# Factors per token spread over the partitions by two small transfers instead of products with the identity

## The chip, the cores and the metric

The kernel runs on one core of a Trainium2 chip. The metric is the device time of one execution in microseconds (us); the time before is 2590.07 us, the median of three runs (2589.15 to 2590.61).

The core has five engines with instruction streams of their own: TensorE (PE in the profile: products of 128-row tiles; PEld is its loading of weights), VectorE (DVE), ScalarE (ACT), GpSimd (POOL) and SyncE (SP). SyncE issues nearly all transfers between memory (DRAM) and the on-chip SBUF. Products land in PSUM, which VectorE and ScalarE read.

## The reference

Two layers on a sequence of 1024 tokens with 1024 features, float32: forgetting attention and then retention, each followed by a gated feed-forward network (FFN), with an RMS norm ahead of each of the four parts and one at the end.

```python
def rmsnorm(x, g):
    y = x * lax.rsqrt(jnp.mean(x * x, axis=-1, keepdims=True) + EPS)
    return y * g

for i in range(2):
    h = rmsnorm(x, norm_mix[i])
    x = x + (forgetting_attention(h, ...) if i == 0 else retention(h, ...))
    h = rmsnorm(x, norm_ffn[i])
    x = x + swiglu(h, ...)
return rmsnorm(x, final_norm)

# retention, per head (4 heads, value width 512), y from the chunked scan:
mu = jnp.mean(y, axis=-1, keepdims=True)
var = jnp.mean(jnp.square(y - mu), axis=-1, keepdims=True)
y = (y - mu) * lax.rsqrt(var + EPS)          # one factor per token
out = (silu(g) * y) @ w_out
```

Each norm has one factor per token, which multiplies that token's whole row of features.

## The kernel before

Activations are kept transposed: features on the 128 partitions, tokens along the free dimension, in two halves of 512 tokens (`HALF`). A factor per token must therefore stand in every partition, as a row of 512 values.

**From sums to factors.** The sum of squares of a token is a product with a column of ones (`colsum`, L159), which puts four blocks of 128 tokens as columns: a tile of 128 x 4 with tokens on the partitions. `rsqrt` takes the factor with a square root on ScalarE, a reciprocal on VectorE and a step of refinement (L144 to L153). `rows` (L165) then turns the column into rows: for each of the four blocks, the column is broadcast to 128 x 128 and multiplied by the identity `ident`, so that each partition gets the same 128 factors. It fills a PSUM tile `rw`. The products are in float32, and each is two records in the trace.

**Who uses it.** `rms` runs in four places: in forgetting attention (fox), in the retention's gates when the first pair comes, and in both FFNs at the first gated tile. Each time, it handles two halves, keeps the factor's column `rcol`, and ScalarE copies `rw` to the SBUF row `R` (L178). The first uses of `R` are L232 in fox, L823 in the FFNs and L964 in the gates. `finish` runs eight times in the retention, for four heads and two halves: it copies the head's output tiles to SBUF (`yt`), sums their squares in `yacc` (L1126), makes the factor `yf` (L1135), and VectorE multiplies the four tiles by `rw` straight from PSUM (L1138). For head 0 it also loads four gate tiles `g` and multiplies by them (L1141, L1142). It stores the tiles to memory as `zd` (L1143), from where the output projection loads them. The final norm calls `rows` too (three times, L874); it is left as it is.

**Around a finish.** The retention goes through eight stages of a head and a half. In each, TensorE computes the next stage's scores (L1074 to L1076) and this stage's weighted values (L1100 to L1102). Every operand of a product is split into a high and a low part (`split`, L98 on ScalarE and L99 on VectorE; the scores also through `atd`, L1085, and `wl`, L1090), and a product is made of three. VectorE also centres the values that come from memory (`vd`, L1011). Tiles of 128 x 512 for such work (`yt`, `sq`, `g`) come from a pool of 16 buffers through `yu`.

**What sets the order.** Every engine runs its own list in order. The lists come from a scheduler, which simulates the program's text before the build, so a change in one place reorders what follows. SyncE's list holds 950 transfers; an entry that waits for its data holds all transfers behind it.

Of the kernel before, what the change touches and what calls it, by code (L numbers as in the profile page):

```python
# [10 lines left out]
F32 = mybir.dt.float32  # L11
# [6 lines left out]
P = 128  # L18
# [19 lines left out]
def trunk(ctx, tc, nc, d, out):  # L38
    cp = ctx.enter_context(tc.tile_pool(name="cp", bufs=1))
    yp = ctx.enter_context(tc.tile_pool(name="yp", bufs=16))  # L40
    dp = ctx.enter_context(tc.tile_pool(name="dp", bufs=1, space=DRAM))
# [10 lines left out]
    R = cp.tile([P, S], F32, tag="R", name="R")  # L52
    cnt = [0]

    def nm(s):
        cnt[0] += 1
        return f"{s}_{cnt[0]}"

    def small(shape, tag, bufs=2):
        return (fp if tag[:2] == "f_" else cp).tile(shape, F32, tag=tag, name=nm(tag), bufs=bufs)  # L60
# [4 lines left out]
    mp = ctx.enter_context(tc.tile_pool(name="mp", bufs=1, space=PSUM))  # L65
    banks = [0]

    def mm_ps():
        tag, n = (("mm", 3), ("st", 2), ("pv", 2), ("mm", 3), ("st", 2), ("pv", 2), ("mm", 3))[banks[0] % 7]
        banks[0] += 1  # L70
        return mp.tile([P, H], F32, tag=tag, name=nm("mm"), bufs=n)

    def yu(s):
        return yp.tile([P, H], F32, tag="y", name=nm(s))
# [35 lines left out]
    HALF = (slice(0, H), slice(H, S))  # L110
# [31 lines left out]
    def rsqrt(v, n, r2=None):  # L142
        sd = small([P, n], "rs_a")
        nc.scalar.activation(sd, v, AF.Sqrt)  # L144
        r = small([P, n], "rs_b")
        nc.vector.reciprocal(r, sd)
        t = small([P, n], "rs_c")
        nc.vector.tensor_tensor(t, r, r, op=ALU.mult)
        nc.vector.tensor_tensor(t, t, v, op=ALU.mult)
        nc.vector.tensor_scalar(t, t, -0.5, 1.5, op0=ALU.mult, op1=ALU.add)  # L150
        if r2 is None:
            r2 = small([P, n], "rs_d")
        nc.vector.tensor_tensor(r2, r, t, op=ALU.mult)  # L153
        return r2

    def colsum(acc, mp, mtag, nb=4):
        ps = mp.tile([P, H], F32, tag=mtag, name=nm("cs"))
        for b in range(nb):
            nc.tensor.matmul(ps[:, b:b + 1], acc[:, b * P:(b + 1) * P], ones[:, 0:1], start=True, stop=True)  # L159
        return ps  # L160

    def rows(col, mp, mtag, nb=4):
        ps = mp.tile([P, H], F32, tag=mtag, name=nm("rw"))
        for b in range(nb):
            nc.tensor.matmul(ps[:, b * P:(b + 1) * P], col[:, b:b + 1].to_broadcast([P, P]), ident,  # L165
                             start=True, stop=True)
        return ps

    def rms(norm, mp, mtag, halves=(0, 1)):
        rc = small([P, TB], "rcol", 2)  # L170
        for h in halves:
            ps = colsum(norm.acc[h], mp, mtag)
            v = small([P, 4], "rv")
            nc.vector.tensor_scalar(v, ps[:, 0:4], 1.0 / D, EPS, op0=ALU.mult, op1=ALU.add)
            rsqrt(v, 4, rc[:, 4 * h:4 * h + 4])
        for h in halves:
            ps = rows(rc[:, 4 * h:4 * h + 4], mp, mtag)
            nc.scalar.copy(R[:, HALF[h]], ps)  # L178
        return rc

    xd = [dp.tile([P, S], F32, tag=f"xd{k}", name=f"xd{k}") for k in range(KT)]
# [3 lines left out]
    with ExitStack() as fs:  # L185
# [232 lines left out]
        for h in range(2):  # L418
            ks.append([fp.tile([P, S], F32R, tag=t, name=nm(t)) for t in ("kh", "kl")])
            for b in range(2):  # L420
                tag, n = (("mm", 3), ("mm", 3), ("st", 2), ("st", 2))[2 * h + b]
# [10 lines left out]
        with tc.issue_after(fed.ins):  # L432
            for kt in range(KT):
                for h in range(2):
                    norm.square(h, x0[kt][h])
        rc = rms(norm, mp, "ms")
        tri = const("tri", [P, P])
        bf = cp.tile([P, FOX_HEADS], F32, tag="bf", name="bf")
# [26 lines left out]
        for i, (n, b) in enumerate(TILES):  # L465
            if i < 3:
                mm_u(ops[n, b], wo[n][6:], last_o[:1], b, first=False, last=(i < EVAC))
            else:
                if n == len(wo):
                    wo.append(wtile(d["fox_o"][n][:, :7 * P], 7))  # L470
                tag, bufs = TAGS[i]
# [30 lines left out]
    class Combos:  # L502
# [27 lines left out]
        def finish(self):  # L530
            for n in self.rest[0]:
                for j in range(4):
                    self.t[n][j] = bsplit(self.pools[n], self.rest[j][n])
# [280 lines left out]
    def ffn(i, X, nrm, xold, xnew, last, nw, pools):  # L814
# [4 lines left out]
        def gated(f, c11, c12, c21, c22):  # L819
            if f == 0:  # L820
                rms(nrm, mp, "ms")
            t = yu("t")
            nc.vector.tensor_tensor(t, c11, R[:, HALF[0]], op=ALU.mult)  # L823
            nc.scalar.activation(t, t, AF.Silu)
            nc.vector.tensor_tensor(c12, c12, R[:, HALF[1]], op=ALU.mult)
            nc.scalar.activation(c12, c12, AF.Silu)
            nc.vector.tensor_tensor(t, c21, t, op=ALU.mult)
            nc.vector.tensor_tensor(c22, c22, c12, op=ALU.mult)
            if f < 16:
                if f % 2 == 0:  # L830
                    even.append((t, c22))
                else:
                    stored[f // 8].put(f % 8 // 2, even.pop(), (t, c22))
                return
            nc.vector.tensor_tensor(t, t, R[:, HALF[0]], op=ALU.mult)
            nc.vector.tensor_tensor(c22, c22, R[:, HALF[1]], op=ALU.mult)
            nc.sync.dma_start(ad[f - 16][:, HALF[0]], t)
            nc.sync.dma_start(ad[f - 16][:, HALF[1]], c22)
# [45 lines left out]
    for n in range(KT):  # L884
# [3 lines left out]
        for b in range(2):  # L888
            if (n, b) in ops:
                ps = ops[n, b]  # L890
            elif n < NPART:
                ps = mp.tile([P, H], F32, tag=("pv", "st")[b], name=nm("mm"), bufs=2)
            else:
                ps = mm_ps()
# [64 lines left out]
    def gates(p, c11, c12, c21, c22):  # L959
        if p == 0:  # L960
            rcs.append(rms(nrm, mp, "ms"))
        for k, h, c in ((0, 0, c11), (0, 1, c12), (1, 0, c21), (1, 1, c22)):
            o = c if h else yu("o")
            nc.vector.tensor_tensor(o, c, R[:, HALF[h]], op=ALU.mult)  # L964
            nc.scalar.activation(o, o, AF.Silu)
            nc.sync.dma_start(gd[2 * p + k][:, HALF[h]], o)
# [24 lines left out]
    rc = rcs[0]  # L991
# [123 lines left out]
    def finish(h, ib, yps):  # L1115
        acc = sp.tile([P, H], F32, tag="sacc", name=nm("yacc"), bufs=2)
        ys = []
        for vt in range(4):
            y = yu("yt")
            nc.scalar.copy(y, yps[vt])  # L1120
            if vt == 0:
                nc.scalar.activation(acc, y, AF.Square)
            else:
                sq = yu("sq")
                nc.scalar.activation(sq, y, AF.Square)
                nc.vector.tensor_tensor(acc, acc, sq, op=ALU.add)  # L1126
            ys.append(y)
        cs = colsum(acc, mp, "ms")
        var = small([P, 4], "yv")
        rs = slice(4 * ib, 4 * ib + 4)  # L1130
        nc.vector.scalar_tensor_tensor(var, cs[:, 0:4], 1.0 / 512, rho2[:, h, rs], op0=ALU.mult, op1=ALU.mult)
        nc.vector.tensor_scalar(var, var, EPS, None, op0=ALU.add)
        r = rsqrt(var, 4)
        fac = small([P, 4], "yf")
        nc.vector.tensor_tensor(fac, r, rho[:, h, rs], op=ALU.mult)  # L1135
        fb = rows(fac, mp, "ms")
        for vt in range(4):
            nc.vector.tensor_tensor(ys[vt], ys[vt], fb, op=ALU.mult)  # L1138
            if h < 1:
                g = yu("g")  # L1140
                nc.sync.dma_start(g, gd[4 * h + vt][:, HALF[ib]])  # L1141
                nc.vector.tensor_tensor(ys[vt], ys[vt], g, op=ALU.mult)  # L1142
            nc.sync.dma_start(zd[4 * h + vt][:, HALF[ib]], ys[vt])  # L1143
# [5 lines left out]
    for i, (h, ib) in enumerate(stages):  # L1149
        nxt = stages[i + 1] if i < 7 else None  # L1150
        if ib == 1 and nxt:
            prepare(h + 1)
        yps = [mm_ps() for _ in range(4)]
        if ib == 1:
            crossed(h, yps)
        an = []
        for dg in range(4):
            if nxt:
                an.append(scores(*nxt, dg))
            weighted(h, ib, dg, a[dg], yps)  # L1160
        a = an
        finish(h, ib, yps)
        if ib == 1 and nxt:
            heads[h + 1][4] = state(heads[h + 1][1], heads[h + 1][3])
# [4 lines left out]
    for n in range(KT):  # L1169
        w = wtile2(d["ret_o"][n], 8)  # L1170
        for h in range(2):
            ps = mm_ps()
# [101 lines left out]
```

## Time and profile before

| | |
|---|---|
| median of three runs | 2590.07 us |
| profiled execution | 2592.81 us |
| its span | 2591.0 us |
| granted TensorE clock | 0.997 |
| TensorE busy | 2562.7 us, 99% |
| VectorE, ScalarE busy | 71%, 47% |

The profile is of one execution. Durations of neighbouring instructions on an engine overlap, above all TensorE's, so the time that one takes is read from its start to the next one's start. A timeline row gives start and duration, and in brackets how long the engine stood idle ahead of it and what released it. A row of the waits gives total, times and longest. In views that group rows, `x` is the number of instructions.

### The profile page before, as it was taken

The numbers are of one execution on the slowest core, as the hardware profiler recorded it, in microseconds if no ns is written. First come the engines' busy times: TensorE is split into PE (matmuls) and PEld (weight loads), VectorE is DVE, ScalarE is ACT, GpSimd is POOL, SyncE is SP. The second block draws the span as 40 slices with busy tenths as digits, with TensorE's granted clock in tenths as the row PEclk, the third lists the DMA queues.
The fourth block names the chain that finished last, engine by engine and source line by source line (L and its number), as shares of the span: only waits on it lengthen the run. The fifth ranks groups of instructions, "written<-read, shape, count | busy, mean of one in ns | idle before, by whom it ended". The sixth has DMA issues, their size and how long they took to land.

```text
span 2591.0 us, 35137 instructions
## 1 busy us (share of the span) xinstructions
PE 2562.7 (99%) x12808; PEld 2184.6 (84%) x12808; DVE 1838.6 (71%) x3131; ACT 1229.5 (47%) x2320; POOL 169.5 (7%) x147
## 2 busy tenths in 40 slices
PE   9999999999999999999999999999999999999998
PEld 8889887888888888889898989898888888888788
DVE  6798888866666768886656576885567666667784
ACT  6566666543333454554343435762354333335543
POOL 0143323000000000001001010000000000000000
PEclk9999999999999999999999999999999999999999
DMA  3111142432332345533332334555522332325441
GB/s 131 44 58 65 51 146 96 149 106 95 113 106 98 127 147 182 161 115 124 102 107 98 122 103 154 191 194 195 195 87 94 105 107 94 110 89 179 167 147 66
DMA packets 137695, 312.12 MB, mean 120 GB/s; under 512 B 15665, under 2 KB 28721, under 8 KB 137521
## 3 DMA queue, kind: packets, MB, share of 16 engines
q1 hardware_dynamic: 136800, 309.33, 35.4%
q8 instruction: 100, 1.64, 0.3%
q14 instruction: 75, 0.61, 0.1%
q10 hardware_dynamic: 720, 0.55, 0.1%
HBM read 217.54 MB, written 92.27 MB: 120 GB/s over the span
## 4 chain that ended last, share of the span: by engine, by line
PE 93%; DVE 2%; issue 1%; DMA 1%; ACT 1%; POOL 0%; DVEq 0%; SPq 0%; POOLq 0%; ACTq 0%
PE mm L635 18%; PE mm L636 18%; PE mm L637 18%; PE mm L106 7%; PE mm L107 7%; PE mm L108 7%; PE mm L751 2%; PE mm L749 2%; PE mm L750 2%; PE mm L256 1%; PE mm L257 1%; PE mm L258 1%; DMA st<-ac_T 1%; PE mm L1101 1%; PE mm L1102 1%
## 5 line engine op out<-in xcount | busy, mean ns | idle before, releaser
L635 PE MATMUL mm<-b,wh 128*128 128x512 f32 x2128 | 827.6, 390 | 5.3 <-ACT 22_4491_22622 L683 3.5
L636 PE MATMUL mm<-b,wh 128*128 128x512 f32 x2128 | 829.3, 390 | 0.0
L637 PE MATMUL mm<-b,wl 128*128 128x512 f32 x2128 | 825.9, 390 | 0.0
L98 ACT CAST wh<-st 128x512 fp32r<-128x512 f32 (+1 forms) x449 | 276.4, 617 | 521.7 <-PE mm L636 318.6
L635 PEld LDWEIGHTS mm<-b,wh 128*128 128x128 f32 x2128 | 400.0, 188 | 88.6 <-ACT 22_4491_22622 L683 4.0
L637 PEld LDWEIGHTS mm<-b,wl 128*128 128x128 f32 x2128 | 400.0, 188 | 83.1
L636 PEld LDWEIGHTS mm<-b,wh 128*128 128x128 f32 x2128 | 400.1, 188 | 82.0
L99 DVE TENSOR_TENSOR wl<-st,wh 128x512 fp32r<-128x512 f32 (+1 forms) x449 | 317.7, 711 | 189.6 <-ACT wh L98 186.1
L98 ACT CAST wh<-s 128x512 fp32r<-128x512 f32 x252 | 156.5, 622 | 306.9 <-PE mm L636 272.9
L106 PE MATMUL mm<-b,wh 128*128 128x512 f32 x736 | 286.5, 392 | 7.7 <-ACT b L126 5.4
L107 PE MATMUL mm<-b,wh 128*128 128x512 f32 x736 | 287.4, 391 | 1.7 <-DVE b L99 1.7
L108 PE MATMUL mm<-b,wl 128*128 128x512 f32 x736 | 287.5, 391 | 0.0
L99 DVE TENSOR_TENSOR wl<-s,wh 128x512 fp32r<-128x512 f32 x252 | 179.8, 715 | 93.3 <-ACT wh L98 89.2
L106 PEld LDWEIGHTS mm<-b,wh 128*128 128x128 f32 x736 | 138.7, 189 | 37.1 <-ACT b L126 6.1
L107 PEld LDWEIGHTS mm<-b,wh 128*128 128x128 f32 x736 | 138.7, 188 | 29.5 <-DVE b L99 2.2
L99 DVE TENSOR_TENSOR b<-st,b 128x512 fp32r<-128x512 f32 x216 | 140.7, 675 | 31.4 <-ACT b L98 28.9
L98 ACT CAST b<-st 128x512 fp32r<-128x512 f32 x216 | 124.5, 611 | 80.9 <-DMA st<-ac_T 26.5
L108 PEld LDWEIGHTS mm<-b,wl 128*128 128x128 f32 x736 | 138.7, 188 | 28.1
L750 PE MATMUL mm<-wl,b 128*128 128x256 f32 x448 | 126.6, 283 | 0.0
L749 PE MATMUL mm<-wh,b 128*128 128x256 f32 x448 | 126.3, 283 | 0.0
L751 PE MATMUL mm<-wh,b 128*128 128x256 f32 x448 | 126.3, 283 | 0.0
L588 DVE TENSOR_TENSOR s<-st 128x512 f32<-128x512 f32 x84 | 58.3, 694 | 65.8 <-DMA st<-ffn_in 27.8
(498 smaller groups left out, 3891.2 us busy)
## 6 DMA issues: line engine op xcount, KB each, us to landing
st<-ffn_in SPq DMA_DIRECT2D x88, 512.0 KB, 3.5
st<-ffn_out_pairs SPq DMA_DIRECT2D x32, 512.0 KB, 4.1
st<-ac_T SPq DMA_DIRECT2D x32, 512.0 KB, 4.8
ac_T<-t SPq DMA_DIRECT2D x48, 256.0 KB, 2.4
st<-ac_B SPq DMA_DIRECT2D x24, 512.0 KB, 4.0
st<-fox_qk SPq DMA_DIRECT2D x32, 256.0 KB, 2.7
xo<-xd SPq DMA_DIRECT2D x32, 256.0 KB, 3.0
ac_B<-t SPq DMA_DIRECT2D x32, 256.0 KB, 2.4
```

The lines of the kernel that those rows point to most:

```text
L98: nc.scalar.copy(hi, src)
L99: return nc.vector.tensor_tensor(lo, src, hi.bitcast(F32), op=ALU.subtract)
L106: nc.tensor.matmul(ps, wh, xh, start=(first and k == 0), stop=False)
L107: nc.tensor.matmul(ps, wh, xl, start=False, stop=False)
L108: nc.tensor.matmul(ps, wl, xh, start=False, stop=(last and k == n - 1))
L588: nc.vector.tensor_tensor(self.s1, self.a21, self.a22, op=ALU.add)
L635: nc.tensor.matmul(ps, hi[:, js], th, start=first and j == 0, stop=False, skip_group_check=True)
L636: nc.tensor.matmul(ps, hi[:, js], tl, start=False, stop=False, skip_group_check=True)
L637: nc.tensor.matmul(ps, lo[:, js], th, start=False, stop=(j == 3), skip_group_check=True)
L749: nc.tensor.matmul(o, th[:, tk], hi[:, js], start=f, stop=False, skip_group_check=True)
L750: nc.tensor.matmul(o, th[:, tk], lo[:, js], start=False, stop=False, skip_group_check=True)
L751: nc.tensor.matmul(o, tl[:, tk], hi[:, js], start=False, stop=(j == 3), skip_group_check=True)
```

## The change

A new function `spread` takes the place of `rows` in `rms` and in `finish`. It issues two transfers on SyncE. The first writes the 128 x 4 column to a small tile in memory, transposed to 4 x 128: 512 single values of four bytes. The second reads these 2 KB into every partition, so that 256 KB land in SBUF. In `rms` they land in `R`, and the copy on ScalarE is gone; the transfers of a half are issued as soon as its factor is computed. In `finish` they land in a tile `fb` from the pool of 16, and VectorE multiplies by that.

```diff
+    def spread(col, dst, nb):
+        m = dp.tile([nb, P], F32, tag=nm("row"), name=nm("row"))
+        nc.sync.dma_start(m.rearrange("b p -> p b"), col)
+        nc.sync.dma_start(dst, m.rearrange("(o b) p -> o (b p)", o=1).to_broadcast([P, nb * P]))
+
     def rms(norm, mp, mtag, halves=(0, 1)):
         rc = small([P, TB], "rcol", 2)
         for h in halves:
...
             rsqrt(v, 4, rc[:, 4 * h:4 * h + 4])
-        for h in halves:
-            ps = rows(rc[:, 4 * h:4 * h + 4], mp, mtag)
-            nc.scalar.copy(R[:, HALF[h]], ps)
+            spread(rc[:, 4 * h:4 * h + 4], R[:, HALF[h]], 4)
         return rc
...
         fac = small([P, 4], "yf")
         nc.vector.tensor_tensor(fac, r, rho[:, h, rs], op=ALU.mult)
-        fb = rows(fac, mp, "ms")
+        fb = yu("fb")
+        spread(fac, fb, 4)
         for vt in range(4):
             nc.vector.tensor_tensor(ys[vt], ys[vt], fb, op=ALU.mult)
```

There are 16 such calls, eight in the norms and eight in the finishes. 64 products go (128 records), 32 transfers come. From `rows` on, the new text's lines stand four to six lower: L1126, L1135, L1138 become L1130, L1139, L1143; L823 becomes L827.

The scheduler moves other work as well. VectorE's list at finish 5, before: the factor `yf`, eight instructions of the scores' splits, then the multiplies by `rw`.

```order
L1135 TENSOR_TENSOR yf_16651<-rs_d_16649,rho_15267 128x4
L1085 SCALAR_TENSOR_TENSOR atd_16867<-mm_16858,kap_15266,mask_15278 128x128
L99 TENSOR_TENSOR wl_16812<-atd_16813,wh_16811 128x128
L1090 SCALAR_TENSOR_TENSOR wl_16812<-mm_16804,kap_15266,wh_16811 128x384
L99 TENSOR_TENSOR wl_16839<-atd_16840,wh_16838 128x128
L1090 SCALAR_TENSOR_TENSOR wl_16839<-mm_16831,kap_15266,wh_16838 128x256
L99 TENSOR_TENSOR wl_16866<-atd_16867,wh_16865 128x128
L1082 CAST wl_16893<-zero 128x128
L1090 SCALAR_TENSOR_TENSOR wl_16866<-mm_16858,kap_15266,wh_16865 128x128
L1138 TENSOR_TENSOR yt_16615<-yt_16615,rw_16653 128x512
```
The same place now:

```order
L1094 SCALAR_TENSOR_TENSOR wl_16843<-mm_16835,kap_15248,wh_16842 128x128
L146 RECIPROCAL rs_b_16621<-rs_a_16619 128x4
L1089 SCALAR_TENSOR_TENSOR atd_16873<-mm_16862,kap_15248,mask_15260 128x128
L148 TENSOR_TENSOR rs_c_16623<-rs_b_16621 128x4
L149 TENSOR_TENSOR rs_c_16623<-rs_c_16623,yv_16616 128x4
L150 TENSOR_SCALAR rs_c_16623<-rs_c_16623 128x4
L99 TENSOR_TENSOR wl_16870<-atd_16873,wh_16869 128x128
L153 TENSOR_TENSOR rs_d_16627<-rs_b_16621,rs_c_16623 128x4
L1139 TENSOR_TENSOR yf_16629<-rs_d_16627,rho_15249 128x4
L1143 TENSOR_TENSOR yt_16593<-yt_16593,fb_16631 128x512
```
The splits now stand ahead of the factor, and nothing is left between `yf` and the multiplies. At the other finishes the list keeps eight, seven, two, six, two, one and two instructions there (finishes 1, 2, 3, 4, 6, 7, 8).

SyncE's list at finish 1, before (`st` are loads of values, `g` of gates, `zd` the stores of the result):

```order
L1007 DMA st_16232<-vd_10889 128x512
L1141 DMA g_15953<-gd_10897 128x512
L1141 DMA g_15958<-gd_10898 128x512
L1143 DMA zd_10913<-yt_15599 128x512
L1141 DMA g_15963<-gd_10899 128x512
L1143 DMA zd_10914<-yt_15602 128x512
L1141 DMA g_15968<-gd_10900 128x512
L1143 DMA zd_10915<-yt_15607 128x512
L1007 DMA st_16238<-vd_10890 128x512
L1143 DMA zd_10916<-yt_15612 128x512
L1007 DMA st_16244<-vd_10891 128x512
```
The same place now:

```order
L1011 DMA st_16211<-vd_10877 128x512
L172 DMA row_15620<-yf_15617 128x4x1
L173 DMA fb_15619<-row_15620 128x512
L1146 DMA g_15624<-gd_10885 128x512
L1146 DMA g_15629<-gd_10886 128x512
L1146 DMA g_15634<-gd_10887 128x512
L1146 DMA g_15639<-gd_10888 128x512
L1011 DMA st_16217<-vd_10878 128x512
L1148 DMA zd_10901<-yt_15581 128x512
L1148 DMA zd_10902<-yt_15584 128x512
L1148 DMA zd_10903<-yt_15589 128x512
L1148 DMA zd_10904<-yt_15594 128x512
```
The two new transfers stand behind the loads of the next keys and ahead of this finish's own gates, which before were loaded earlier (those before in the first list belong to finish 2); the second load of values moved ahead of the stores.

VectorE's list in the first FFN where `R` is first used, before:

```order
L99 TENSOR_TENSOR wl_5787<-st_5580,wh_5786 128x512
L99 TENSOR_TENSOR wl_5804<-s_1177_5691,wh_5803 128x512
L589 TENSOR_TENSOR s_1228_5983<-s_1227_5982,st_5915 128x512
L672 TENSOR_TENSOR u_1141_5512<-mm_5497,u_1141_5512 128x512
L99 TENSOR_TENSOR wl_5848<-s_1203_5843,wh_5847 128x512
L823 TENSOR_TENSOR t_5681<-mm_5496,R 128x512
```
And now:

```order
L99 TENSOR_TENSOR wl_5775<-st_5574,wh_5774 128x512
L99 TENSOR_TENSOR wl_5792<-s_1181_5679,wh_5791 128x512
L827 TENSOR_TENSOR t_5669<-mm_5490,R 128x512
L593 TENSOR_TENSOR s_1232_5971<-s_1231_5970,st_5903 128x512
L831 TENSOR_TENSOR t_5669<-mm_5492,t_5669 128x512
L676 TENSOR_TENSOR u_1143_5506<-mm_5491,u_1143_5506 128x512
```
The first multiply by `R` moved ahead of a sum of weights, a sum of results and a split.

## The prediction

> **What bounds the kernel now.** I read the page first (busy times, then the chain that ended last), then TensorE's waits, then the broadcast's tile.
>
> ```profile
> PE 2562.7 (99%) x12808; PEld 2184.6 (84%) x12808; DVE 1838.6 (71%) x3131; ACT 1229.5 (47%) x2320; POOL 169.5 (7%) x147
> ...
> PE 93%; DVE 2%; issue 1%; DMA 1%; ACT 1%; POOL 0%; DVEq 0%; SPq 0%; POOLq 0%; ACTq 0%
> ```
> TensorE is busy for 99% of the span and carries 93% of the chain, so time taken off its queue comes off the end, if nothing new makes it wait. It hardly waits now; the largest row of its waits:
>
> ```profile
> PE mm L106 <- ACT b L126: 5.4, 1, 5.4
> ```
> The tile `rw` is what the removed products write. In its view (duration min/median/max in ns, first and last start), the `rcol` rows are the RMS norms and the `yf` rows the eight retention finishes; below them, who waited for them.
>
> ```profile
> L165 PE MATMUL rw<-ident,rcol x64: 271/275/276, 46.4 to 1965.2; 128*128 128x128 f32 x64
> L165 PE MATMUL rw<-ident,yf x64: 270/275/276, 1638.6 to 1778.7; 128*128 128x128 f32 x64
> L178 ACT COPY R<-rw x8: 586/587/591, 47.5 to 1965.5; 128x512 f32<-128x512 f32 x8
> ...
>   DVE yt L1138: 3.7, 3
> ```
>
> **The products that go.** TensorE's timeline at finish 1 shows one call, eight records on one row:
>
> ```profile
> 1638.59 1.05 PE L165 MATMUL rw<-ident,yf 128*128 128x128 f32 x8
> 1639.40 0.48 PE L1049 MATMUL mm<-b,b 128*128 128x512 f32 x1
> 1639.71 0.39 PE L1050 MATMUL mm<-b,b 128*128 128x512 f32 x1
> 1639.94 0.40 PE L1051 MATMUL mm<-b,b 128*128 128x512 f32 x1
> ```
> Durations overlap, so I count from start to start: 1639.40 − 1638.59 = 0.81 us until the next product starts, and that product keeps the array 0.31 us where its neighbour keeps it 0.23. A call costs 0.81 + 0.08 = 0.89 us. 64 + 64 records by 8 are 16 calls: 16 × 0.89 = **14.2 us less on TensorE**, half in the norms, half in the finishes. The eight `R` copies (8 × 0.587 = 4.7 us) leave ScalarE, busy 47%: I count nothing. VectorE's multiplies read `fb` from SBUF instead of PSUM; the same count, at the duration that the multiplies by `g` show (0.64 us each in a pair, against 2.47 / 4 = 0.62): nothing.
>
> **How late the factor comes.** Now SyncE issues the store of the column, waits for it to land, and issues the load. No transfer of 2 KB in single elements is in the trace, so I bound it. The views of the transfers give microseconds from issue to landing:
>
> ```profile
> xd<-x SPq DMA_DIRECT2D x16, 256.0 KB, 3.8
> ...
> st<-vd SPq DMA_DIRECT2D x32, 256.0 KB, 3.3
> zd<-yt SPq DMA_DIRECT2D x32, 256.0 KB, 2.8
> ...
> st<-ret_o SPq DMA_DIRECT2D x32, 256.0 KB, 3.0
> ...
> xd<-y SPq DMA_DIRECT2D x16, 256.0 KB, 2.0
> ...
> st<-qd SPq DMA_DIRECT2D x8, 512.0 KB, 6.1
> ...
> st<-fox_v SPq DMA_DIRECT2D x12, 256.0 KB, 2.5
> ```
> Store: 2.0 (fastest) to 3.8 (slowest of these 256 KB stores). Load: 2.5 to 6.1. With 0.3 us for two hand-overs (an estimate) the delay L from `yf` to the first multiply by `fb` lies between 4.8 and 10.2 us. I take 2.8 + 3.1 + 0.3 = **6.2 us**: `zd<-yt` is the store of the same finishes on the same queue, 3.1 is between the two loads of the retention, and SyncE, held by the wait, puts nothing between the two transfers.
>
> The Trainium skill ("DMA: Bandwidth & Descriptors", "Anatomy of one DMA") gives a fixed 2.0 us per transfer, most of it the write's receipt, plus bytes over 436 GB/s. By it L would be 2.0 + 2.6 + 0.3 = 4.9 us; the rows above are longer for the same 256 KB.
>
> **The norms' halves (8 calls).** Their factor is used long after it is known. VectorE's timeline, second half's `rcol` and first use of `R` in each of the four norms, and what surrounds the use in the first FFN:
>
> ```profile
> 44.89 0.16 DVE L153 TENSOR_TENSOR rcol<-rs_b,rs_c 128x4 f32<-128x4 f32 x1
> ...
> 63.74 0.68 DVE L232 TENSOR_TENSOR qf<-mm,R 128x512 f32<-128x512 f32 x1
> ...
> 509.67 0.16 DVE L153 TENSOR_TENSOR rcol<-rs_b,rs_c 128x4 f32<-128x4 f32 x1
> ...
> 514.43 0.69 DVE L589 TENSOR_TENSOR s<-s,st 128x512 f32<-128x512 f32 x1
> 516.63 0.69 DVE L672 TENSOR_TENSOR u<-mm,u 128x512 f32<-128x512 f32 x1 [1.50 <-PE mm L637]
> ...
> 1152.52 0.15 DVE L153 TENSOR_TENSOR rcol<-rs_b,rs_c 128x4 f32<-128x4 f32 x1
> ...
> 1172.89 0.68 DVE L964 TENSOR_TENSOR o<-mm,R 128x512 f32<-128x512 f32 x1
> ...
> 1953.10 0.16 DVE L153 TENSOR_TENSOR rcol<-rs_b,rs_c 128x4 f32<-128x4 f32 x1
> ...
> 1960.61 0.68 DVE L823 TENSOR_TENSOR t<-mm,R 128x512 f32<-128x512 f32 x1
> ```
> Between are 18.9 and 20.4 us in fox and the gates, 7.5 us in the second FFN: more than L. The first FFN is the tight one, because the new order puts the multiply by `R` ahead of L589: `R` lands at about 509.83 + 6.2 = 516.0, VectorE gets there at 514.4 and stands 1.6 us. What is queued behind (`s`, `u`, one weight split) slips by that and the multiply itself; the 1.50 us in which VectorE stood idle there anyway pay for most of it. Cost: nothing. If the cover is gone (L over 9), a weight split is late there and TensorE waits 1 to 3 us. So of the norms' 7.1 us I keep all.
>
> **The finishes (8 calls).** Here VectorE works in order and stands at the first multiply by `fb`, with the splits for TensorE's next products behind it. The stretch as a whole (length, then busy us of PE, PEld, DVE, ACT, POOL) and the place after finish 1 and around finish 5, VectorE's timeline and then one row of TensorE's:
>
> ```profile
> 1630.00:1785.00 155.00, 153.29 (x884) 137.07 (x883) 121.66 (x286) 88.25 (x191) 0.00 (x0) 1.00 0.57 194
> ```
> ```profile
> 1640.17 2.47 DVE L1138 TENSOR_TENSOR yt<-yt,rw 128x512 f32<-128x512 f32 x4
> ...
> 1643.16 1.28 DVE L1142 TENSOR_TENSOR yt<-yt,g 128x512 f32<-128x512 f32 x2
> ...
> 1654.75 0.75 DVE L1011 SCALAR_TENSOR_TENSOR b<-st,vmean,b 128x512 fp32r<-128x512 f32 x1 [2.90 <-ACT b L1010]
> ```
> ```profile
> 1715.83 0.15 DVE L1135 TENSOR_TENSOR yf<-rs_d,rho 128x4 f32<-128x4 f32 x1
> ...
> 1718.96 2.48 DVE L1138 TENSOR_TENSOR yt<-yt,rw 128x512 f32<-128x512 f32 x4 [0.74 <-PE rw L165]
> ...
> 1723.21 0.69 DVE L1126 TENSOR_TENSOR yacc<-yacc,sq 128x512 f32<-128x512 f32 x1
> ```
> ```profile
> 1728.34 0.83 PE L159 MATMUL cs<-ones,yacc 128*128 128x1 f32 x7
> ```
> VectorE's idle time there, 155 − 121.66 = 33.3 us, is all that can swallow the freezes. Two leads can be read: 2.9 us idle after finish 1, and 1728.34 − 1723.90 = 4.4 us from the last sum to its product after finish 5. I use their mean, 3.6 us, at each finish (a choice: the leads elsewhere are not on one row).
>
> The freeze is L less the VectorE work that the new order leaves between `yf` and the multiplies. From start to start a centring of the values (L1011) takes 0.67 us and a full-width sum 0.61, here at finish 3:
>
> ```profile
> 1683.57 0.75 DVE L1011 SCALAR_TENSOR_TENSOR b<-st,vmean,b 128x512 fp32r<-128x512 f32 x1
> 1684.24 0.68 DVE L1126 TENSOR_TENSOR yacc<-yacc,sq 128x512 f32<-128x512 f32 x1
> 1684.85 0.68 DVE L99 TENSOR_TENSOR b<-mm,b 128x512 fp32r<-128x512 f32 x1
> ```
> With 0.6 for a full-width split, and 0.4 and 0.2 to 0.4 for those of half and of quarter width (estimates by their width), the new order's cover is 2.7, 3.7, 1.3, 3.3, 0, 1.8 and 0.6 us at finishes 1 to 7; finish 8 is beside the output projection and is left out. At L = 6.2 the freezes are 3.5, 2.5, 4.9, 2.9, 6.2, 4.4, 5.6 us; less the lead: 0, 0, 1.3, 0, 2.6, 0.8, 2.0, **6.7 us of new waits**, the largest at finish 5, where no work is left in between. The same sum gives 2 us at L = 4.9, 11.9 at 7.2, 18.8 at 8.2 and 25.8 at 9.2. The gain is used up at L = 7.5.
>
> SyncE stands too, some 3 us per finish, until the store has landed. Behind it at finish 1 are the four loads of `g` and a load of the values; SyncE's own timeline:
>
> ```profile
> 1646.43 0.41 SPq L1007 DMA_DIRECT2D st<-vd  x1
> ...
> 1655.53 0.32 SPq L1007 DMA_DIRECT2D st<-vd  x1
> ```
> The first of these two now stands ahead of the `zd` stores and can go once the `g` loads are issued, at about 1643; the second stays behind the stores and went 9 us after the first, so stores that are 4 us late don't reach it. I count nothing for the queue; if that cover is gone, the values come late and the freeze after finish 1 grows by as much. The bytes are 16 loads of 256 KB more, where `zd` alone has 32 stores of that size: nothing.
>
> **Sum.** −14.2 + 6.7 = −7.5 us. Against the profiled execution (2592.81 us, span 2591.0) that is 2585.3; it stands 2.7 us above the median of 2590.07, so for the median **2582.6 us**.
>
> **Rivals.**
> - *All of it hidden*: L near 4.9, so that the leads hold nearly everywhere: −14.2 + 2 = −12.2, 2578; with no wait at all 2575.9. For it: VectorE idles 33 us in the stretch. Against it: finish 5 leaves no work in between. The skill's 2.0 us rule would give this outcome.
> - *A draw*: L = 7 to 8, freezes of 10 to 17 us eat the finishes' share and the norms' 7.1: 2586 to 2593, taken as 2589. For it: the stretch has much traffic (DMA share 0.57 in its row), and the first transfer queues behind earlier loads.
> - *Slower*: the store of 512 single elements is slow by itself. From L = 8.3 on (2.1 us more than I take) the loss passes 14.2 + 5.2; at L = 9.2, a store of 5.8 us, it is 25.8 − 14.2 = +11.6, 2601.7. For it: no row shows that such a store is as quick as one of long rows. Against it: it moves 2 KB, not 256. The skill's page, under "Rules for kernel authors", says that a strided last dimension becomes one descriptor per element and should be rearranged; it states no price for so small a one, and no run before shows any.
>
> **How the numbers follow.** A measurement of this kernel tells about 0.2%, 5.2 us, from no change. Faster by more needs new waits under 9 us, L under 6.8: my forecast 0.32 and the hidden case 0.20, together 0.52. The draw 0.26, slower 0.22. The range leaves out the fully hidden end and the slow store's tail: 2576 to 2600; the forecast's own is 2578 to 2586.
>
> **What would show it.** No `rw` rows from `rcol` or `yf`; TensorE's busy time 14 us less; two SyncE transfers per call, the store 2.8 us and the load 3.1 from issue to landing; a VectorE wait of 2.5 to 6 us on a DMA ahead of the `yt<-yt,fb` rows, longest at finish 5; new TensorE waits of 5 to 9 us in the stretch from 1605 to 1785 and none at the norms. I am wrong if the store takes over 5 us, if the leads are shorter than 3.6 us, or if VectorE's stand reaches the weights' splits in the FFN.

## The result, and the profile after

The changed kernel takes 2657.96 us (median of five runs, 2657.39 to 2665.4) against 2589.98 before: a ratio of 1.0272 (95% interval 1.026 to 1.0283), 68 us slower. The forecast was 2582.6, the range 2576 to 2600. The profiled execution is the slowest of the five, 2665.4 us with a span of 2663.6; it is set against the profiled span of before, 2591.0: 72.6 us.

The page after: the busy times, the row of TensorE's clock in tenths per slice of the span, and the chain that ended last:

```profile
PE 2576.0 (97%) x12680; PEld 2187.1 (82%) x12680; DVE 1836.2 (69%) x3131; ACT 1224.6 (46%) x2312; POOL 171.2 (6%) x147
...
PEclk9999999999999999999999999888999999999999
...
PE 82%; DMA 8%; DVE 5%; issue 2%; ACT 2%; SPq 0%; POOL 0%; DVEq 0%; POOLq 0%; ACTq 0%
```
128 records are gone and TensorE is busy for 13 us more, not 14 less: in three slices of the retention it has a lower clock (the 8s). Transfers now have 8% of the chain, where they had 1%. The view of the transfers, from issue to landing:

```profile
R<-row SPq DMA_DIRECT2D x8, 256.0 KB, 4.3
...
fb<-row SPq DMA_DIRECT2D x8, 256.0 KB, 5.4
row<-rcol SPq DMA_DIRECT2D x8, 2.0 KB, 10.0
row<-yf SPq DMA_DIRECT2D x8, 2.0 KB, 8.1
```
The store of 2 KB takes 8 to 10 us, where I had taken 2.8 and drawn the bound at 3.8. At finish 5, SyncE's timeline and VectorE's:

```profile
1769.49 0.37 SPq L172 DMA_DIRECT2D row<-yf  x1
1777.55 0.32 SPq L173 DMA_DIRECT2D fb<-row  x1
```
```profile
1769.30 0.16 DVE L1139 TENSOR_TENSOR yf<-rs_d,rho 128x4 f32<-128x4 f32 x1
1782.48 2.50 DVE L1143 TENSOR_TENSOR yt<-yt,fb 128x512 f32<-128x512 f32 x4 [13.02 <-DMA fb<-row]
```
The load is issued when the store has landed, 8.06 us after it, and VectorE stands 13.02 us; from `yf` to the multiply L is 1782.48 − 1769.30 = 13.2 us. Over all eight finishes and two FFNs (VectorE's waits), and what that does to TensorE (its three largest waits of 26 rows):

```profile
DVE yt L1143 <- DMA fb<-row: 79.5, 8, 13.0
...
DVE t L827 <- DMA R<-row: 16.9, 2, 9.7
```
```profile
PE mm L1079 <- DVE b L99: 11.8, 2, 6.0
PE mm L1078 <- DVE b L99: 9.5, 2, 5.3
PE cs L159 <- DVE yacc L1130: 7.2, 1, 7.2
```
The rows of TensorE's waits add up to 22.1 us before and 81.0 after. The clock has its own part. Stretches of the changed kernel: the first at finish 2, the second at finish 3, the third at the second FFN's norm, the last at the first norm; and under them the whole retention (columns as in the prediction; the clock is the third number from the end):

```profile
1700.60:1707.40 6.80, 4.38 (x10) 3.47 (x11) 6.80 (x12) 2.35 (x4) 0.00 (x0) 0.50 0.99 336
1707.50:1728.00 20.50, 15.36 (x87) 13.63 (x85) 8.49 (x26) 8.84 (x20) 0.00 (x0) 1.00 0.40 122
2042.00:2045.40 3.40, 3.40 (x9) 2.65 (x8) 3.40 (x7) 2.36 (x5) 0.00 (x0) 0.50 0.00 0
...
72.60:79.20 6.60, 4.92 (x12) 4.11 (x13) 5.65 (x16) 2.38 (x4) 0.00 (x0) 0.50 0.29 93
```
```profile
1640.00:1870.00 230.00, 183.55 (x902) 158.11 (x901) 127.12 (x295) 96.69 (x206) 0.00 (x0) 0.90 0.48 145
```
Each wait of TensorE of 2.3 us or more has a stretch at half clock in it or behind it here, of 3.4 or 6.8 us, once (from 1844 on, at the wait of 7.2) of 10.2. Over the span the granted clock is 0.986, against 0.997 before: 0.014 x 2663.6 − 0.003 x 2591.0 = 29.5 us of full clock lost. So the 72.6 us are about 58.9 of new waits, 29.5 of clock, less the 14.2 of the products: 74.2. The sum is 1.6 too high: the clock is rounded, and half clock during a wait is counted twice. The Trainium skill ("TensorE: Matmul & The Clock Gate", "Part 1: The HAM clock gate") states that an idle window of about 3.4 us sets the clock to half. The lengths above agree, in steps of 3.4 us; the condition doesn't quite: waits of 2.4 us (up to 533.6) and 2.3 us (up to 1816.6) have a stretch at half clock behind them too, from 533.3 and 1816.7 on.

Where it lies, by the lag of TensorE's products behind the same products before (the n-th product with the removed ones left out of both traces): 9.0 us after the first norm, of which 1.3 come back within the attention; 4.2 more at the first FFN's norm, 5.4 at the gates, 57.5 in the finishes, 3.4 at the second FFN's norm, and 5 back late in the last FFN, where before has a wait that this kernel hasn't (shown below).

### The profile page after: what moved, and what is told of

The parts are those of the page before. It is cut to its first block, busy times and chain, and to the rows that moved or that the text cites. A ratio compares the mean times of both kernels' runs of the same rounds, so it can differ in the third digit from the quotient of the medians.

```text
span 2663.6 us, 34912 instructions
## 1 busy us (share of the span) xinstructions
PE 2576.0 (97%) x12680; PEld 2187.1 (82%) x12680; DVE 1836.2 (69%) x3131; ACT 1224.6 (46%) x2312; POOL 171.2 (6%) x147
## 4 chain that ended last, share of the span: by engine, by line
PE 82%; DMA 8%; DVE 5%; issue 2%; ACT 2%; SPq 0%; POOL 0%; DVEq 0%; POOLq 0%; ACTq 0%
PE mm L639 17%; PE mm L640 17%; PE mm L641 17%; PE mm L106 6%; PE mm L108 6%; PE mm L107 6%; DMA row<-yf 2%; PE mm L755 2%; PE mm L753 2%; PE mm L754 2%; DMA row<-rcol 2%; DMA fb<-row 1%; PE mm L260 1%; PE mm L261 1%; PE mm L262 1%
## 5 line engine op out<-in xcount | busy, mean ns | idle before, releaser
L639 PE MATMUL mm<-b,wh 128*128 128x512 f32 x2128 | 829.6, 391 | 11.5 <-DVE u L671 5.1
```

Source lines behind the costliest of these rows:

```text
L639: nc.tensor.matmul(ps, hi[:, js], th, start=first and j == 0, stop=False, skip_group_check=True)
```

## The experiments

Two theories at the start. The one: the factor is late, VectorE stands, and the splits behind it are late for TensorE. The rival: SyncE, held until the store has landed, keeps TensorE's operands late. A third came up on the way: the store itself makes other transfers late. The kernel before ran beside each group; its medians were 2589.0 to 2590.1.

**The two halves of the change apart.** `norms_only` has `fb = rows(fac, mp, "ms")` in `finish`; `finishes_only` has the old loop with `rows` and the copy in `rms`.

> The norms' eight halves go through memory, the finishes keep their products. TensorE's product-by-product lag of the changed kernel behind the one before grew by 7.6 us at the first norm, 4.2 at the second, 5.4 at the third, 3.4 at the fourth. If each place pays by itself (theory: the factor is late by store plus load, about 13.5 us), this kernel is 14 to 21 us over before: 2604 to 2611. If the norms' lag came from the finishes' queue or from a lower clock behind them (rival), it is within 5 us of before.

Measured 2604.26, ratio 1.0056 (1.0041 to 1.0071): +14.2 us.

> Only the eight finishes go through memory. If each place pays by itself: the lag between 1640 and 1810 us of the changed kernel, 57.5 us, stands alone: 2644 to 2650. If the two halves work together (rival: transfers of the norms disturb the rest), less than 45 us over before.

Measured 2645.36, ratio 1.0216 (1.02 to 1.0231): +55.3 us. The sum, 69.5, is the whole change, 68: each place pays by itself, and the norms too, where I had expected a gain of 7.1.

How the norms pay is not the same in all four. In the FFNs VectorE stands for `R`, 12.0 us in two waits. In the attention SyncE's hold does it. Its timeline in `norms_only`, with the halves' two stores one behind the other, then what ScalarE and TensorE waited for:

```profile
50.52 0.43 SPq L172 DMA_DIRECT2D row<-rcol  x1
61.84 0.32 SPq L173 DMA_DIRECT2D R<-row  x1
62.25 10.48 SPq L84 DMA_DIRECT2D st<-fox_qk  x4
```
```profile
67.54 0.62 ACT L98 CAST wh<-st 128x512 fp32r<-128x512 f32 x1 [11.74 <-DMA st<-fox_qk]
```
```profile
74.31 1.11 PE L332 MATMUL st<-qh,kh 128*128 128x512 f32 x2 [7.65 <-ACT qh L98]
```
The loads of weights (`fox_qk`) could go only when the second store had landed, 11.3 us after its issue; before, the same loads went from 55.73 on:

```profile
55.73 7.82 SPq L84 DMA_DIRECT2D st<-fox_qk  x4
```
At the gates it is the load of `ret_v` that goes when the second store has landed:

```profile
1189.24 0.69 DVE L592 TENSOR_TENSOR s<-st 128x512 f32<-128x512 f32 x1 [9.81 <-DMA st<-ret_v]
```
TensorE then waits 5.5 us. No wait for `R` shows at these two places.

**The multiplies later.**

```diff
-        spread(fac, fb, 4)
-        for vt in range(4):
-            ...
+        spread(fac, fb, 4)
+        if late:                       # the finish before this one
+            with tc.issue_after(known.ins):
+                late()
+        return multiply                # the loop, called by the next finish
```

> Both transfers stay as in the changed kernel, at the same places and on the same queue; the four multiplies by the factor, with the gates and the store, stand one finish later, behind the next factor on VectorE, so that VectorE does not stand while the factor travels. Theory (VectorE stands, and the splits behind it are late): the finishes' 57.5 us go and their products' 7.1 us come off: 2590 to 2600, with the norms' 20 us left in it. Rival (SyncE held for 8 us per store keeps TensorE's operands late): within 10 us of the changed kernel, 2645 to 2660.

Measured 2649.05, ratio 1.0233 (1.0209 to 1.0256): 9 us less than the change, and inside the rival's range. It isn't a clean answer: VectorE's stand for `fb` went from 79.5 us to 11.7, but the gates' loads now stood behind the next store on SyncE, and VectorE stood 15.6 us for them:

```profile
1693.74 1.32 DVE L1152 TENSOR_TENSOR yt<-yt,g 128x512 f32<-128x512 f32 x2 [8.51 <-DMA g<-gd]
```
But the values came late too, as in the changed kernel, ahead of any such load. SyncE's and ScalarE's timelines of the changed kernel at finish 1:

```profile
1652.27 0.32 SPq L1011 DMA_DIRECT2D st<-vd  x1
1654.60 0.37 SPq L172 DMA_DIRECT2D row<-yf  x1
```
```profile
1661.83 0.72 ACT L1014 ACTIVATE b<-st,vmean 128x512 fp32r<-128x512 f32 x1 [5.28 <-DMA st<-vd]
```
A load of values issued 2.3 us ahead of the store was there only 9.5 us after its issue; before, the loads of values take 3.3 (median; the longest 7.5). That is neither theory.

**Longer rows.**

```diff
+        ps = mp.tile([P, H], F32, tag="ms", name=nm("rw"))
+        nc.tensor.matmul(ps[0:nb, 0:P], col, ident, start=True, stop=True)
+        rt = dst[0:nb, 0:P]
+        nc.scalar.copy(rt, ps[0:nb, 0:P])
-        nc.sync.dma_start(m.rearrange("b p -> p b"), col)
+        nc.sync.dma_start(m, rt)
```

> As the changed kernel, but the column is first turned into four rows by one product with the identity and one copy on ScalarE, and the store writes four rows of 512 bytes instead of 512 values of 4 bytes; the load is the same. Theory (the store's single values are what takes 8 us): the store lands in 2 to 3 us, the delay falls from 13.5 to about 9, and the sum of the prediction gives 26 us of waits in the finishes: 2600 to 2615. Rival (any store with a load behind it takes this long): the store still lands after 7 us or more, and the time is over 2640.

Measured 2603.86, ratio 1.0055 (1.004 to 1.007), 54 us less than the change. The view of the tile `row` gives the first and the last start of each transfer:

```profile
L176 SPq DMA_DIRECT2D row<-R x8: 260/264/331, 45.2 to 1987.4; - x8
L177 SPq DMA_DIRECT2D R<-row x8: 319/332/411, 46.4 to 1988.6; - x8
L176 SPq DMA_DIRECT2D row<-fb x8: 260/262/270, 1638.3 to 1805.4; - x8
L177 SPq DMA_DIRECT2D fb<-row x8: 319/320/376, 1640.0 to 1807.4; - x8
```
At these starts the load follows 1.2 to 2.0 us behind the store, for whose landing it waits: the 8 us belong to the single values, not to the trip through memory. The lag is −3.6 us ahead of the retention; the finishes add 19.2, where the factor now passes TensorE and ScalarE on its way.

**SyncE free, then VectorE too.** `pool_load` is `finishes_only` with `nc.gpsimd.dma_start(dst, ...)` for the load; `pool_load_deferred` adds the later multiplies, with the gates' loads ahead of the spread; `long_pool_deferred` adds the long rows.

> As finishes_only (2645), but the load of the spread factor is issued by GpSimd, which has nothing else to do there: SyncE issues the store and goes on. VectorE stands as before. If VectorE's stand is the cause, 2635 to 2655. If SyncE's hold is the cause, 20 us or more less: under 2625.

Measured 2658.75, ratio 1.0269 (1.0253 to 1.0284). With SyncE free it is 13 us slower than `finishes_only`, so freeing SyncE alone gains nothing in the finishes. It isn't clean either: SyncE now issues other transfers while the store is under way, and the gates' loads land after 12.2 us instead of 5.3 (medians of `g<-gd`), the store after 9.2 instead of 8.1. Which of these makes it slower was not followed.

> As pool_load, and the multiplies stand one finish later on VectorE, with the gates' loads ahead of the spread: neither VectorE nor SyncE stands for the factor, but the store of single values is still there. If the two stands are all: 2581 to 2588, the products' 7.1 us gained. If the store by itself makes other transfers late (in the changed kernel a load of values issued 2.3 us ahead of a store landed after 9.5 us, against 3.5 to 4.3 for its neighbours): 2600 or more.

Measured 2618.65, ratio 1.0114 (1.0099 to 1.0129): 40 us less than `pool_load`, 27 less than `finishes_only`; VectorE stood for 79.8 us and now for 11.5. So VectorE's stand is a good part of the finishes' cost; how large is not shown, since the gates' loads moved as well. And 29.6 us over before are left with hardly anything standing for the factor, though 7.1 of products are saved: the store costs something by itself.

> As pool_load_deferred, with the column turned into four rows by one product and the store of four rows of 512 bytes. All three suspects are gone: 2583 to 2590 (of 7.1 us some 2 go back to the eight products). If a round trip through memory costs by itself, 2600 or more.

Measured 2595.55, ratio 1.0027 (1.0018 to 1.0037). Long rows take away another 23 us. It is 5.5 us above the expected range. Of the products' 7.1 us the eight new ones take back 2.5 (0.31 each, from the start of one to the start of what follows it); what the other waits of some 6 us in the retention are was not followed.

**128 pieces instead of 512.**

```diff
-        nc.sync.dma_start(m.rearrange("b p -> p b"), col)
+        nc.sync.dma_start(m.rearrange("b (q e) -> (b q) e", e=nb), col)
```

> As the changed kernel in all 16 places, but the store writes the column as it stands, 128 runs of 16 bytes instead of 512 of 4; the factors then belong to other tokens, which leaves out the transposition. If the store's price goes by the number of its pieces (about 6 of its 8 us), it lands after 3.5 us and the time is 2600 to 2620, as with long rows. If it goes by the bytes or is a fixed price for pieces under some length, it still lands after 7 us and the time is 2650 to 2665.

Measured 2590.06, ratio 1.0005 (0.9996 to 1.0014): the whole loss is gone by this one line, and the time is below both forecasts. The views of its transfers, of VectorE's wait, and of the retention's stretch:

```profile
R<-row SPq DMA_DIRECT2D x8, 256.0 KB, 3.6
...
fb<-row SPq DMA_DIRECT2D x8, 256.0 KB, 4.0
row<-rcol SPq DMA_DIRECT2D x8, 2.0 KB, 2.4
row<-yf SPq DMA_DIRECT2D x8, 2.0 KB, 2.6
```
```profile
DVE yt L1143 <- DMA fb<-row: 26.9, 8, 5.5
```
```profile
1640.00:1870.00 230.00, 218.78 (x1080) 186.91 (x1079) 151.33 (x314) 100.96 (x208) 0.00 (x0) 0.97 0.60 198
```
The same 2 KB land in 2.4 to 2.6 us. With L = 2.6 + 4.0 + 0.3 = 6.9, near the 6.2 of the prediction, TensorE's lag ahead of the retention is −7.0 us (six calls at 0.89 are 5.3, and some 1.5 came in the attention), the fourth norm gives −1.9 (two calls: 1.8), and the finishes in between add 10.9, with a clock of 0.97 in the stretch. The 1.5 us are not the transfers': there the profile of before has 3.4 us at half clock from 395.5 on and this one none, and `extra_store` (below), whose attention is that of before, has the same gain.

**The store alone.** The kernel before, with one store more per finish that nothing reads; in the second kernel each value has 64 bytes to itself.

```diff
         fb = rows(fac, mp, "ms")
+        m = dp.tile([4, P], F32, tag=nm("row"), name=nm("row"))
+        nc.sync.dma_start(m.rearrange("b p -> p b"), fac)
# or
+        m = dp.tile([4, P, 16], F32, tag=nm("row"), name=nm("row"))
+        nc.sync.dma_start(m[:, :, 0].rearrange("b p -> p b"), fac)
```

> The kernel before, with the products, plus one store in each finish: the factor's column to memory as 512 values of 4 bytes, as the changed kernel does, read by nothing. Nothing in the program waits for it but the end and the reuse of a small buffer two finishes later. Theory (the store itself makes the other transfers land late, the values above all): 10 to 35 us over before, 2600 to 2625. Rival (only those who wait for the factor pay): within 4 us of before.

Measured 2600.65, ratio 1.0047 (1.0031 to 1.0062): +11.4 us for eight stores for which nothing waits (the profiled execution, the fastest of its runs, has a span 5.2 us over that of before; its lag grows by 9.0 us in the retention). The transfers' view, and ScalarE's wait for the values, 20.5 us before:

```profile
st<-vd SPq DMA_DIRECT2D x32, 256.0 KB, 4.0
zd<-yt SPq DMA_DIRECT2D x32, 256.0 KB, 5.5
...
row<-yf SPq DMA_DIRECT2D x8, 2.0 KB, 9.0
```
```profile
ACT b L1010 <- DMA st<-vd: 32.1, 18, 5.0
```
The stores of the finishes land after 5.5 us, where before they took 2.8.

> As extra_store, but each of the 512 values goes to a place of its own, 64 bytes from the next. If the price is that sixteen values share 64 bytes of memory: the store lands in under 4 us and the time is within 4 us of before. If it is the number of small writes: the store lands after 7 us or more and the time is as extra_store's.

Measured 2589.43, ratio 0.9998 (0.9989 to 1.0007), no difference, and no lag in the retention:

```profile
st<-vd SPq DMA_DIRECT2D x32, 256.0 KB, 3.7
zd<-yt SPq DMA_DIRECT2D x32, 256.0 KB, 2.5
...
row<-yf SPq DMA_DIRECT2D x8, 2.0 KB, 2.9
```
```profile
ACT b L1010 <- DMA st<-vd: 21.2, 16, 4.6
```
As many pieces, as short, from the same partitions (both pages count 19888 packets under 512 bytes, that of before 15665): 9.0 us where their targets lie side by side, 2.9 where they lie 64 bytes apart. Neither the number of pieces nor their length makes the price by itself; it comes when 4-byte pieces lie side by side in memory. Pieces of 16 bytes that lie side by side (`runs_of_16`) don't have it. Which distance or which length is enough was not tried, and what in the memory or the transfer engines makes the price is not shown.

**What is left to gain.** The norms by 16-byte runs, turned back by ScalarE's copy; then the finishes as well.

```diff
-            spread(rc[:, 4 * h:4 * h + 4], R[:, HALF[h]], 4)
+        m = dp.tile([P, nb], F32, tag=nm("row"), name=nm("row"))
+        nc.sync.dma_start(m, col)
+        t = yu("rt")
+        nc.sync.dma_start(t, m.rearrange("(o p) b -> o (p b)", o=1).to_broadcast([P, nb * P]))
+        nc.scalar.copy(dst.rearrange("q (b p) -> q b p", b=nb), t.rearrange("q (p b) -> q b p", b=nb))
```

> The norms' halves go through memory by a store of 128 runs of 16 bytes (2.5 us in runs_of_16) and a load; ScalarE's copy to R reads the loaded tile with a stride, so that the tokens stand right. The finishes keep their products. In runs_of_16 TensorE's lag after the norms was -7.0 us, so 2589.5 - 7 = 2582 to 2583 (2579 to 2586). If the copy's strided read or its wait brings back the late factor: 2588 or more.

Measured 2577.84, ratio 0.9957 (0.9945 to 0.997): 11.4 us less than before, the fastest here, and 1.2 us below the expected range. Its busy times and the transfers' view:

```profile
PE 2551.8 (99%) x12744; PEld 2173.9 (84%) x12744; DVE 1836.9 (71%) x3131; ACT 1231.0 (48%) x2320; POOL 169.6 (7%) x147
```
```profile
rt<-row SPq DMA_DIRECT2D x8, 256.0 KB, 4.4
...
row<-rcol SPq DMA_DIRECT2D x8, 2.0 KB, 1.9
```
The products' 7.1 us are in it: the lag is −6.8 ahead of the retention, and the fourth norm gives −1.9. A further 5 us come late in the last FFN, where before has this wait and, in the stretch around it, a lower clock, and this kernel's profile has neither; that part was not aimed at, and no run shows that the transfers bring it.

```profile
PE mm L635 <- ACT 22_4491_22622 L683: 3.5, 1, 3.5
```
```profile
2425.00:2440.00 15.00, 11.46 (x44) 9.05 (x43) 10.15 (x17) 8.23 (x16) 0.00 (x0) 0.89 0.59 202
```

> Norms as in norms_runs; the finishes too by runs of 16 bytes, the load issued by GpSimd, and the multiplies one finish later, reading the factor with a stride. All products are gone (14.2 us). If no stand is left: 2576. With the 6 us of other waits that long_pool_deferred showed in the finishes: 2580 to 2584. If a store of 16-byte runs disturbs other transfers as that of single values does: over 2590.

Measured 2583.3, ratio 0.9977 (0.9968 to 0.9986), inside the 2580 to 2584 for a kernel with other waits: the lag is −6.2 us ahead of the retention and grows by 4.3 in it. The finishes give no gain even so.

## Why the prediction was wrong

- **The products: right.** 0.89 us per call; two calls gave −1.9 us at the fourth norm in `runs_of_16` and in `norms_runs`, where 1.8 were worked out. The copies on ScalarE and the SBUF operand cost nothing that shows.
- **The delay L: the step that failed.** "I take 2.8 + 3.1 + 0.3 = **6.2 us**." It was 8.1 + 5.4 in the finishes, 13.2 us from `yf` to the multiply at finish 5, and 10 us for the store alone in the norms. The 0.3 us for the hand-overs came from no row; at finish 5 0.19 us pass from the start of `yf` to the issue of the store. The nearest row was chosen by place and queue, not by form: each of the rows used as bounds moved 256 KB or more, in rows of 2 KB or more, and the store of the change wrote 4 bytes 512 times into 2 KB. The bound of 3.8 was none for that; a store of over 5 us, named as a sign of being wrong, is what came. The rival *slower* had the mechanism, but stopped at a store of 5.8 us, and the range with it. The Trainium skill ("DMA: Bandwidth & Descriptors", "Rules for kernel authors") says that a strided last dimension becomes one descriptor per element and should be rearranged; the advice was right here, but the number of pieces alone isn't the price: in `extra_store_apart` they are as many, and land in 2.9 us.
- **The norms at no cost: wrong.** In `norms_only` they cost 14.2 us: 13.8 of waits (35.9 − 22.1), 7.8 of clock (0.006 x 2604.2 − 7.8), less 7.1. In the FFNs the step is L. In the attention and at the gates the 18.9 and 20.4 us until `R` is used would have covered an L of 14 to 15; what the prediction left out there is that SyncE stands for two stores in a row and issues the loads behind them late. TensorE's two waits there are 7.7 and 5.5 us. It is the same slow store in both cases: with one of 2.4 us (`runs_of_16`) the norms' gain comes.
- **The finishes' sum: the form held, the clock was missing.** At L = 13.2 the freezes less cover are 79.0 us for seven finishes; VectorE stood 67.0 us there (79.5 with the eighth), and at finish 1 5.8 us more, for values that came late. Less 3.6 each, the sum gives 53.8 us of waits, where TensorE's rows of that stretch add up to 46. What the sum had no term for is the half clock around each long wait: 0.10 x 230 = 23 us in the stretch. 46 + 23 − 7.1 is 62, near the 57.5 of the lag. `runs_of_16` is the test near the L that was assumed: at 6.9 the sum gives 10.1 us of waits, TensorE's rows in the retention add up to 11.1, and the clock (0.03 x 230) adds 7. So by this estimate the forecast would have been some 7 us too low even with a quick store.
- **SyncE's hold at nothing: wrong in the norms, open in the finishes.** In the norms it has the two waits above. In the finishes `pool_load` frees SyncE and gains nothing, but sends the gates' loads out beside the slow store; in `deferred` the hold made VectorE stand for the gates.
- **Bytes at nothing: the wrong measure.** It is not the bytes of the store but the time that it holds others up.

What stays open: why `pool_load_deferred` keeps 29.6 us over before when the store alone costs 11.4 in the kernel before, and how the remaining waits of the deferred kernels come about.

## What to carry to other kernels

Price a transfer by its form, not its bytes: when no row of the trace has the form (short pieces, a transposed target), measure that transfer alone before the sum rests on it, and let the range reach as far as not knowing it demands. Ask not only who waits for the data but what stands behind the transfer in the issuing engine's list. Turn a small column on the side of the reader (a strided copy in SBUF) and let the store write its runs as they stand. Where TensorE is the bound, price the clock with the wait: here 58.9 us of new waits came with 29.5 us of lost clock, half as much again.

## What the runs showed of the hardware

A store of 512 values of 4 bytes that lie side by side in memory landed after 8 to 10 us (medians); with the values 64 bytes apart after 2.9; with 128 runs of 16 bytes, side by side, after 1.9 to 2.8. The Trainium skill ("DMA: Bandwidth & Descriptors", "Specifications") says that pieces under 512 bytes are read, modified and written; here pieces of 4 and of 16 bytes both came near the 2.0 us that "Anatomy of one DMA" of that page gives for transfers issued from GpSimd, except the 4-byte pieces side by side (all these stores were issued from SyncE). While the slow store was under way, a load issued ahead of it on the same queue landed after 9.5 us (median before 3.3, longest 7.5), and in `extra_store` the finishes' stores landed after 5.5 us instead of 2.8. And in the changed kernel TensorE's clock stood at half for 3.4 to 10.2 us in or behind each of its waits of 2.3 us and more, which took 29.5 us of full clock more than before over the span (0.014 of it, against 0.003).
